# A four-layer decoder trunk on one core: the layer turns and the end of the last layer, written in another order

## The chip, the cores and the metric

The kernel runs on one core of a Trainium2 chip. The metric is the device time of one execution in microseconds (us), the median of several runs. A core has five instruction streams that run side by side and wait for each other by semaphores: PE (TensorE, matrix products and transposes), DVE (VectorE), ACT (ScalarE), POOL (GpSimd) and SP (which here only issues DMAs); ACT and POOL issue DMAs as well. Products of PE land in PSUM, eight banks of 128 x 512 words; everything else lies in SBUF.

## The reference

One sequence of 512 tokens, width 1024, runs through a recurrent (RG-LRU) layer, a PEER expert layer, a multi-head latent attention (MLA) layer, a second PEER layer and a last norm:

```
x = x + gate * rglru(norm(x)*(1+scale)+shift)
x = x + gate * peer(norm(x)*(1+scale)+shift)      # layer 0
k_nope, k_rope, v = shared_kv(x)                  # w_dkv (256), w_kr, latent norm, w_uk, w_uv
x = x + gate * mla(norm(x)*(1+scale)+shift)       # w_dq (384), latent norm, w_uq, 16 heads, w_o
x = x + gate * peer(norm(x)*(1+scale)+shift)      # layer 1
out = rmsnorm(x, final_g)
```

A norm is x * rsqrt(mean(x*x) + eps). PEER makes 8 queries per token (w_pq), takes the top 16 of 128 x 128 product keys for each, and sums over the chosen experts gate * gelu(h . u[e]) * v[e].

## The kernel before, in words

**Layout.** The residual x is kept transposed: 8 tiles k of 128 features by 512 tokens. Every 32-bit product is done as three products of a high and a low half (`mm3`, L188 to L190: weight low by activation high, weight high by activation low, high by high); `split` (L161, L162) makes the halves, the high one as a copy on ACT, the low one as a difference on DVE or POOL. `wtile` loads a weight tile on SP's queue into `raw` and splits it; tiles `whi`, `wlo` come from a small pool, `xhi`, `xlo` from one of the stage. A scheduler orders each engine's stream by its own costs; `tc.issue_after(i)` forces what is inside it behind instruction i.

**A norm** has four steps. `sum_sq` (L221) squares a tile of x on ACT (L226) and adds it to `nacc` on DVE or POOL (L227); `col_sums` (L233) multiplies nacc by ones on PE, one column for each 128 tokens, tile `st`; `rstd_row` takes the square root on ACT (L244), the reciprocal on DVE (L245), and four transposes on PE (L248) that spread it over all partitions, tile `rs`; `normed` (L258) multiplies x by rs, and `affine` (L266 to L274) applies scale and shift, giving `hf` in full and the two halves (`h` in the expert layers, `hmh` and `hml` in attention).

**Stages and turns.** `run` calls `rglru`, `peer(0)`, `mla`, `peer(1)` and `final`. `rglru` ends with the products `wo`, a residual (L283) and the squares. `peer` starts with the norm, three banks `pq` filled k by k with three weight tiles split on DVE, further `pq` groups and scores `sc` (L971). Then two ways are taken: 384 of the tokens go through all 16384 experts densely (tiles u, L188 to L190, with gelu, and gates by the products `wps` of L863, which wait for `pr` on DVE), the last 128 through gathers of the chosen rows (L1169 to L1178). In the value phase 128 steps t add v tiles to the six accumulators `acc` (3 token blocks by 2 halves); the last three steps (`LAST`) are held back and worked off by `emit`, `finish` and the adds of L1143, which turn the token rows `onat` back into columns by PE transposes `ot` (L1121), add the residual and square. In peer two of the eight banks are set apart ("side").

**`mla`** starts with a norm for the keys and one for the queries from the same rs, products `lat` (w_dkv, two tiles) and then `kr` (w_kr), then three more `lat` tiles (w_dq) for the queries. `latent_sums` copies the latents (`latr`), squares them and sums; `latent_norm` (L551) makes ckv and qlat in halves; `values` (v) and `keys` (kn) follow, and per head `q`, `qf` (L654), scores and softmax, `pv` (L695 to L703), and the output products `wo` in four groups g.

**`final`** (L1186) norms x by feature tiles and stores eight tiles of 128 x 512 (L1192, L1193); the host transposes.

## Time and profile before

| | us |
|---|---|
| median of 3 runs | 3069.69 (3067.85 to 3071.66) |
| the profiled execution's own time | 3070.86 |
| its span | 3069.1 |
| PE busy | 2975.9 |
| DVE busy | 2553.9 |
| ACT busy | 1372.3 |
| POOL busy | 899.9 |
| mean granted PE clock | 0.986 |

The profile is of one execution: its span runs from the first to the last instruction, its own time has a little more around it. Rows of groups give a line, an engine, result <- inputs, shapes, the count, then busy time, mean ns of one and the idle time ahead with what ended it. Rows of the timeline give the start, the length, engine, line, operation, and in brackets the engine's wait ahead of it. PE's clock is the share of full speed that the throttle granted.

### The profile page before, as it was taken

To read this page: it belongs to the slowest core of one execution; us is meant where nothing else is said; L and a number is where in the kernel's file an instruction comes from. 1 tells how busy PE (TensorE), PEld (TensorE's weight loads), DVE (VectorE), ACT (ScalarE), POOL (GpSimd) and SP (SyncE) were. 2 spreads that over 40 slices of the span, in tenths; PEclk is the share of its full clock that TensorE was granted. 3 is DMA by queue.
4 is the path that set the end of the run, shared out by engine and by line. 5 is a ranking of instruction groups with operands and counts; after the bars stand their busy time and mean duration, and the time that the engine had idled before them with its cause. 6 is when DMAs were issued, how large, how long until landed. Compare 5 with 4: busy or idle time off the path is not lost.

```text
span 3069.1 us, 43439 instructions
## 1 busy us (share of the span) xinstructions
PE 2975.9 (97%) x15516; PEld 2640.9 (86%) x15516; DVE 2553.9 (83%) x4839; ACT 1372.3 (45%) x1967; POOL 899.9 (29%) x705
## 2 busy tenths in 40 slices
PE   7989999999999999999899989999999999999998
PEld 5679999999888889998677779999999888899986
DVE  8979999898698878879667778999897877788887
ACT  5742255655343333333466642456554333333333
POOL 4000004343224234545333300024342521144441
PEclk9999999999999999999899999999999999999999
DMA  8444568899989999999113344379999999999994
GB/s 311 163 154 145 182 209 311 292 355 317 356 306 378 365 324 350 323 342 328 51 52 121 95 163 130 125 237 325 318 337 330 363 347 331 320 307 353 323 332 145
DMA packets 297209, 814.74 MB, mean 265 GB/s; under 512 B 32864, under 2 KB 131296, under 8 KB 290592
## 3 DMA queue, kind: packets, MB, share of 16 engines
q1 hardware_dynamic: 188912, 438.89, 42.1%
q0 software_dynamic: 78912, 287.34, 26.6%
q10 hardware_dynamic: 29168, 85.72, 7.2%
q8 instruction: 123, 2.02, 0.3%
q14 instruction: 94, 0.77, 0.1%
HBM read 727.70 MB, written 84.15 MB: 265 GB/s over the span
## 4 chain that ended last, share of the span: by engine, by line
PE 74%; DVE 12%; DMA 7%; issue 4%; ACT 2%; POOL 1%; SPq 0%; DVEq 0%; ACTq 0%; POOLq 0%
PE u L188 9%; PE acc L189 9%; PE u L190 9%; PE u L189 9%; PE acc L190 9%; PE acc L188 9%; PE wps L863 5%; DMA vraw<-in_v_dram 3%; DVE wlo L162 2%; DMA ada_raw<-in_adaw_dram 1%; PE pq L188 1%; PE pq L190 1%; PE pq L189 1%; PE ri L415 1%; DVE ada_junk L150 1%
## 5 line engine op out<-in xcount | busy, mean ns | idle before, releaser
L188 PE MATMUL u<-h,wlo 128*128 128x384 f32 x2048 | 691.9, 338 | 1.3 <-ACT gact L928 1.0
L190 PE MATMUL u<-h,whi 128*128 128x384 f32 x2048 | 687.5, 336 | 0.0
L189 PE MATMUL u<-h,whi 128*128 128x384 f32 x2048 | 686.3, 335 | 0.0
L1169 POOL DMA_INDIRECT grow<-in_u_dram,idx x256 | 351.4, 1373 | 1084.2 <-DVE gdot L1173 403.2
L189 PE MATMUL acc<-vl,ah 128*128 128x512 f32 x1536 | 597.8, 389 | 2.7 <-DVE vl L162 2.5
L190 PE MATMUL acc<-vh,ah 128*128 128x512 f32 x1536 | 597.8, 389 | 0.0
L1169 POOL DMA_INDIRECT grow<-in_v_dram,idx x256 | 379.3, 1481 | 652.3 <-DVE gacc L1178 345.7
L188 PE MATMUL acc<-vh,al 128*128 128x512 f32 x1536 | 557.4, 389 | 4.0 <-ACT vh L161 3.4
L162 DVE TENSOR_TENSOR wlo<-raw,whi 128x1024 fp32r<-128x1024 f32 x313 | 382.1, 1222 | 108.4 <-ACT whi L161 108.3
L162 DVE TENSOR_TENSOR vl<-vraw,vh 128x1024 fp32r<-128x1024 f32 x256 | 313.1, 1223 | 144.0 <-ACT vh L161 143.6
L161 ACT ACTIVATE whi<-raw 128x1024 fp32r<-128x1024 f32 (+2 forms) x370 | 356.2, 963 | 149.2 <-issue 38.6
L188 PEld LDWEIGHTS u<-h,wlo 128*128 128x128 f32 x2048 | 386.3, 189 | 5.6 <-ACT gact L928 1.7
L189 PEld LDWEIGHTS u<-h,whi 128*128 128x128 f32 x2048 | 385.6, 188 | 2.7
L190 PEld LDWEIGHTS u<-h,whi 128*128 128x128 f32 x2048 | 385.1, 188 | 0.0
L188 PEld LDWEIGHTS acc<-vh,al 128*128 128x128 f32 x1536 | 288.1, 188 | 64.4 <-ACT vh L161 5.2
L189 PEld LDWEIGHTS acc<-vl,ah 128*128 128x128 f32 x1536 | 288.6, 188 | 61.9 <-DVE vl L162 3.4
L190 PEld LDWEIGHTS acc<-vh,ah 128*128 128x128 f32 x1536 | 288.7, 188 | 59.4
L1178 DVE SCALAR_TENSOR_TENSOR gacc<-grow,gdot,gacc 128x1024 f32<-128x1024 f32 x254 | 325.0, 1279 | 14.6 <-DMA grow<-in_v_dram,idx 13.4
L161 ACT ACTIVATE vh<-vraw 128x1024 fp32r<-128x1024 f32 x256 | 268.7, 1051 | 131.4 <-issue 63.8
L1173 DVE CUSTOM_DVE_ANT_0 grow<-grow,hn 128x1024 f32<-128x1024 f32 x256 | 309.6, 1220 | 16.2 <-DMA grow<-in_u_dram,idx 16.2
L161 ACT ACTIVATE ah<-gact 128x384 fp32r<-128x384 f32 x204 | 106.7, 523 | 361.4 <-PE acc L190 189.2
L863 PE MATMUL wps<-pr,oo 128*128 128x128 f16 x1536 | 191.0, 297 | 14.9 <-DVE pr L856 14.7
(359 smaller groups left out, 4211.5 us busy)
## 6 DMA issues: line engine op xcount, KB each, us to landing
raw<-in_uT_dram SPq DMA_DIRECT2D x256, 512.0 KB, 5.2
vraw<-in_v_dram SPq DMA_DIRECT2D x256, 512.0 KB, 6.2
wscr<-stg ACTq DMA_DIRECT2D x48, 1024.0 KB, 6.6
wt<-wscr SPq DMA_DIRECT2D x14, 3072.0 KB, 19.8
ada_raw<-in_adaw_dram SPq DMA_DIRECT2D x76, 512.0 KB, 4.5
gscr<-gsp ACTq DMA_DIRECT2D x136, 192.0 KB, 5.2
gact<-gscr SPq DMA_DIRECT2D x112, 192.0 KB, 6.6
ada_raw<-in_adaw_dram POOLq DMA_DIRECT2D x36, 512.0 KB, 6.5
```

The source lines that it names most:

```text
L150: nc.vector.tensor_tensor_reduce(junk, raw, self.csil, op0=OP.mult, op1=OP.add, scale=1.0, scalar=b, accum_out=col)
L161: last = nc.scalar.activation(hi, src, AF.Copy)
L162: lo = (eng or nc.vector).tensor_tensor(lo, src, hi.bitcast(F32), op=OP.subtract)
L188: nc.tensor.matmul(out, al, bh, start=first, stop=False)
L189: nc.tensor.matmul(out, ah, bl, start=False, stop=False)
L190: return nc.tensor.matmul(out, ah, bh, start=False, stop=last)
L415: nc.tensor.matmul(out, w[:, q, :], xc[2 * hd + k], start=k == 0, stop=k == 1)
L863: last = nc.tensor.matmul(wps[:, t * P:t * P + P], oo[:, n4 + a, :, t], pr[:, q * n4 + a, :, t], start=q == 0, stop=q == 1)
L1169: nc.gpsimd.indirect_dma_start(out=row, out_offset=None, in_=tabs[s], in_offset=bass.IndirectOffsetOnAxis(ap=idx[:, k:k + 1], axis=0))
L1173: nc.vector.tensor_tensor_reduce(row, row, hn, op0=OP.mult, op1=OP.add, scale=1.0, scalar=0.0, accum_out=col)
L1178: nc.vector.scalar_tensor_tensor(acc, row, col, acc, op0=OP.mult, op1=OP.add)
```

## The change

In the order of the program:

- **Squares and constant products at the turns to peer and mla.** `sum_sq` gets `parts`: the squares of the last two tiles go into a tile `nsq` and are not added to nacc; `col_sums` multiplies nacc and both parts by ones, three times four columns, in an order forced by hand. `fill` puts constant products (128 x 512, f16, of the table iota_e) into PE's stream, ahead of the sums, ahead of the transposes of rs and behind them: 4, 2 and 7 at the two turns to peer, 2, 2 and 7 at the turn to mla. The first products of the stage are held behind the last of them. The three first w_pq tiles are split one after the last residual, one after the last square too, one after the reciprocal and the square root.
- **Entry of attention.** The two w_dkv tiles are loaded and split at the end of peer 0. The three products lat, lat, kr take k in turn; the next xn stands ahead of each low half. Squares of the latents are taken from PSUM, ahead of the copies. The kv sums come after all of lats[1], the third query tile is done in two halves with the transposes of rs between, the query sums stand between the halves of values(0), and their rs ahead of keys(0). The first w_uq and w_uk tiles are split early, on DVE; rope's memset goes from DVE to POOL; the load of the Exp table is later.
- **Exit of attention.** project_out(3) is held behind the last pv product; the last head pair is split on DVE, not POOL.
- **End of layer 1.** `token_major` turns x and the gate g2 into token rows during the value phase (40 transposes on PE, 10 copies on ACT; csil's memory takes the gate). final_g is loaded as rows. `close` works the held steps off block by block: multiply by the gate and add x on DVE, squares with a running sum on ACT, root, reciprocal, product with final_g, and a store of 512 KB of token rows per block, the last one in two halves on two queues. The output is (512, 1024) rows; `final` goes.

```diff
@@ -225,0 +229,7 @@
+        if k >= n - parts:
+            if not self.parts:
+                self.pair_sq = self.wp.tile([P, 2, T], F32, name="nsq", tag="raw", bufs=RAWS)
+            part = self.pair_sq[:, len(self.parts), :]
+            self.parts.append(part)
+            self.last_sq = nc.scalar.activation(part, ch, AF.Square).ins
+            return self.last_sq
@@ -230,6 +240,5 @@
+    def fill(self, bank, n):
+        e = self.iota_e.rearrange("p e t -> p (e t)")
+        for _ in range(n):
+            with self.tc.issue_after(self.tail):
+                self.tail = self.nc.tensor.matmul(bank, e[:, :P], e, start=True, stop=True).ins
@@ -237,3 +246,17 @@
-    def rstd(self, n):
-        self.col_sums()
-        return self.rstd_row(n)
+    def col_sums(self, warm=None):
+        self.sums = self.bank("st")
+        parts, last = [*self.parts[:1], self.nacc, *self.parts[1:]], None
+        if warm:
+            self.fill(self.sums, warm[0])
+            last = self.tail
+        for i, part in enumerate(parts):
+            for b in range(NB):
+                with self.tc.issue_after(last) if last is not None else ExitStack():
+                    last = self.nc.tensor.matmul(self.sums[:, b:b + 1], part[:, b * P:b * P + P], self.ones,
+                                                 start=i + b == 0, stop=i == len(parts) - 1, skip_group_check=True).ins
+        self.tail = last
+        return last
+
+    def rstd(self, n, warm=None):
+        self.col_sums(warm)
+        return self.rstd_row(n, warm)
@@ -248 +273,5 @@
-            nc.tensor.transpose(rs[:, b * P:b * P + P], col[:, 1, b:b + 1].to_broadcast([P, P]), self.ident)
+            with self.tc.issue_after(self.tail) if warm else ExitStack():
+                t = nc.tensor.transpose(rs[:, b * P:b * P + P], col[:, 1, b:b + 1].to_broadcast([P, P]), self.ident)
+        self.tail = t.ins
+        if warm:
+            self.fill(self.sums, warm[2])
@@ -569 +604,3 @@
-            rs = self.rstd(D)
+            last_res, last_sq = self.last_res, self.last_sq
+            rs = self.rstd(D, (2, 2, 7))
+            warm = self.tail
@@ -573,2 +613,4 @@
-                    xn.append(self.normed(hp, k, rs))
-                    hk.append(self.affine(hp, k, xn[k], gk, self.mod[:, 96:104])[1])
+                    step = None
+                    if k + 1 < KC:
+                        step = lambda: xn.append(self.normed(hp, k + 1, rs))
+                    hk.append(self.affine(hp, k, xn[k], gk, self.mod[:, 96:104], between=step)[1])
@@ -577,4 +619,5 @@
-                outs = [self.bank("lat"), self.bank("lat"), self.bank("kr")]
-                self.lin_k(outs[:2], [self.wtile(io["w_dkv"][m], KC, eng=nc.vector) for m in range(2)], hk)
-                self.lin(outs[2], self.wtile(io["w_kr"], KC, eng=nc.vector), hk)
-                wdq = [self.wtile(io["w_dq"][m], KC, pool=hp) for m in range(2)]
+                    with tc.issue_after(warm) if k == 0 else ExitStack():
+                        for out, (hi, lo) in zip(outs, (*self.wdkv, wkr)):
+                            self.mm3(out, (hi[:, k, :], lo[:, k, :]), hk[k], k == 0, k == KC - 1)
+                with tc.issue_after(self.last_sqrt):
+                    wdq = [self.wtile(io["w_dq"][m], KC, pool=hp) for m in range(2)]
@@ -593,4 +636,11 @@
-                with tc.issue_after(self.latent_sums(pool, outs[:2])):
-                    self.lin(lats[1], wdq[1], hq)
-                self.latent_norm("kv_latent_g", ckv)
-                self.lin(lats[2], self.wtile(io["w_dq"][2], KC), hq)
+                self.latent_squares(pool, outs[:2])
+                with tc.issue_after(self.lin(lats[1], wdq[1], hq)):
+                    self.col_sums()
+                w2 = self.wtile(io["w_dq"][2], KC)
+                with tc.issue_after(self.tail):
+                    half = self.lin(lats[2], w2, hq, range(4))
+                with tc.issue_after(half):
+                    rs = self.rstd_row(2 * P)
+                self.latent_norm("kv_latent_g", ckv, rs)
+                with tc.issue_after(self.tail):
+                    whole = self.lin(lats[2], w2, hq, range(4, KC))
@@ -634,2 +684,9 @@
-            values(0)
-            self.latent_sums(top, lats)
+            w0 = self.wtile(io["w_uq"][0], 3, eng=nc.vector)
+            wk0 = self.wtile(io["w_uk"][0], 2, eng=nc.vector)
+            sq = self.latent_squares(top, lats, 1)
+            with tc.issue_after(whole), tc.issue_after(sq):
+                values(0, (0,))
+            with tc.issue_after(self.tail):
+                self.col_sums()
+            with tc.issue_after(self.tail):
+                values(0, (2,))
@@ -743,2 +803,3 @@
-                project_out(3, m)
-                self.sum_sq(pool.tile([P, T], F32, name="sq", tag="t"), self.x[:, m, :], m)
+                with tc.issue_after(self.last_pv):
+                    project_out(3, m)
+                self.sum_sq(pool.tile([P, T], F32, name="sq", tag="t"), self.x[:, m, :], m, parts=2)
@@ -888 +950,3 @@
-                with tc.issue_after(last_nacc), tc.issue_after(last_sq) if m else ExitStack():
+                with ExitStack() as order:
+                    for ins in ((last_res,), (last_res, last_sq), (self.recip, self.last_sqrt))[m]:
+                        order.enter_context(tc.issue_after(ins))
@@ -1100,0 +1170,8 @@
+                if l == DEPTH - 1 and t >= 26 and (t - 26) % 8 == 0 and (t - 26) // 8 <= KC:
+                    with tc.issue_after(grp["v"]):
+                        self.token_major((t - 26) // 8, g2)
+                if l == DEPTH - 1 and t == P - 12:
+                    fg = hpool.tile([P, D], F32, name="fgrow", tag="h4")
+                    with tc.issue_after(vdma[t]):
+                        nc.sync.dma_start(fg, bass.AP(tensor=io["final_g"].tensor, offset=io["final_g"].offset,
+                                                      ap=[[0, P], [1, D]]))
@@ -1106,2 +1186,4 @@
+            if l == 0:
+                with tc.issue_after(vls[-1]), tc.issue_after(self.last_split[0]):
+                    self.wdkv = [self.wtile(io["w_dkv"][m], KC, eng=nc.vector) for m in range(2)]
@@ -1147,0 +1230,62 @@
+    def token_major(self, k, g2):
+        nc = self.nc
+        if k < KC:
+            ot = self.bank("ot", True)
+            for b in range(NB):
+                nc.tensor.transpose(ot[:, b * P:b * P + P], self.x[:, k, b * P:b * P + P], self.ident)
+            nc.scalar.activation(self.x[:, k, :], ot, AF.Copy)
+            return
+        for f in range(2):
+            ot = self.bank("ot", True)
+            for i in range(NB):
+                nc.tensor.transpose(ot[:, i * P:i * P + P], g2[:, f * NB + i:f * NB + i + 1].to_broadcast([P, P]), self.ident)
+            nc.scalar.activation(self.csil[:, f * T:f * T + T], ot, AF.Copy)
+
+    def close(self, pool, acc, held, gathered, fg, splits):
+        nc, tc, io = self.nc, self.tc, self.io
+        nd = NB - 1
+        ys = [pool.tile([P, D], F32, name=f"y{b}", tag=f"h{b}") for b in range(NB)]
+        sq = pool.tile([P, 2, T], F32, name="sqy", tag="h5")
+        st = self.consts.tile([P, NB, 5], F32, name="ssum")
+
+        def add(b, f, src):
+            y = ys[b][:, f * T:f * T + T]
+            nc.vector.tensor_tensor(y, src, self.csil[:, f * T:f * T + T], op=OP.mult)
+            y4 = y.rearrange("p (k n) -> p k n", n=P)
+            last = nc.vector.tensor_tensor(y4, y4, self.x[:, f * NB:f * NB + NB, b * P:b * P + P], op=OP.add).ins
+            nc.scalar.activation(sq[:, f, :], y, AF.Square, accum_out=st[:, b, f:f + 1])
+            if f == 0:
+                nc.vector.tensor_scalar(st[:, b, 2:3], st[:, b, 0:1], 1.0 / D, EPS, op0=OP.mult, op1=OP.add)
+            else:
+                nc.scalar.activation(st[:, b, 3:4], st[:, b, 1:2], AF.Sqrt, bias=st[:, b, 2:3], scale=1.0 / D)
+                nc.vector.reciprocal(st[:, b, 4:5], st[:, b, 3:4])
+            return last
+
+        def out(b, after, parts=1):
+            n = D // parts
+            for i in range(parts):
+                cs = slice(i * n, i * n + n)
+                with tc.issue_after(after):
+                    nc.vector.scalar_tensor_tensor(ys[b][:, cs], ys[b][:, cs], st[:, b, 4:5], fg[:, cs],
+                                                   op0=OP.mult, op1=OP.mult)
+                (nc.scalar if i else nc.sync).dma_start(io["out"][b * P:b * P + P, cs], ys[b][:, cs])
+
+        self.preload(AF.Sqrt, self.last_split[0])
+        last = None
+        for f in range(2):
+            with tc.issue_after(splits[0]), tc.issue_after(splits[1]):
+                after = add(nd, f, gathered[:, f * T:f * T + T])
+        out(nd, after)
+        for b in range(nd):
+            bs = slice(b * P, b * P + P)
+            for f in range(2):
+                fs = slice(f * T, f * T + T)
+                for t, (a, v) in held:
+                    with tc.issue_after(last) if last is not None else ExitStack():
+                        last = self.mm3(acc[b][f], (a[0][:, bs], a[1][:, bs]), (v[0][:, fs], v[1][:, fs]), False,
+                                        t == P - 1).ins
+                after = add(b, f, acc[b][f])
+                if b and f == 0:
+                    out(b - 1, after)
+        out(nd - 1, after, 2)
+
```

Three places in the engines' streams. DVE at the turn from the recurrent layer to peer 0 (`raw` is a loaded weight, wlo and xlo its low half, rcol the reciprocal, xn the normed tile), before:

```order
L227 TENSOR_TENSOR nacc<-nacc,sq 128x512 x3
L162 TENSOR_TENSOR wlo<-raw,whi 128x1024 x3
L162 TENSOR_TENSOR xlo<-raw,xhi 128x1024
L245 RECIPROCAL rcol<-rcol 128x4
L258 TENSOR_TENSOR xn<-x,rs 128x512
L268 TENSOR_SCALAR hf<-xn,gs_f_1540,mod 128x512
```

and after:

```order
L237 TENSOR_TENSOR nacc<-nacc,sq 128x512
L162 TENSOR_TENSOR wlo<-raw,whi 128x1024
L268 RECIPROCAL rcol<-rcol 128x4
L162 TENSOR_TENSOR wlo<-raw,whi 128x1024
L287 TENSOR_TENSOR xn<-x,rs 128x512
L162 TENSOR_TENSOR xlo<-raw,xhi 128x1024
L297 TENSOR_SCALAR hf<-xn,gs_f_1539,mod 128x512
```

Two adds to nacc are gone; the reciprocal stands behind one low half where it stood behind four, and the first xn behind two.

PE in attention, round the query latents' sums (v are value products, kn key products, st the sums), before:

```order
L190 MATMUL v<-wuvh,ckvh_13684 128x256
L233 MATMUL st<-ones,nacc 128x1 x4
L188 MATMUL kn<-ckvh_13682,wlo 128x512
L189 MATMUL kn<-ckvl_13683,whi 128x512
L190 MATMUL kn<-ckvh_13682,whi 128x512
L188 MATMUL kn<-ckvh_13684,wlo 128x512
L189 MATMUL kn<-ckvl_13685,whi 128x512
L190 MATMUL kn<-ckvh_13684,whi 128x512
L248 MATMUL rs<-ident,rcol 128x128 x4
L188 MATMUL q<-qlh_13686,wlo 128x512
```

and after:

```order
L188 MATMUL v<-wuvh,ckvl_13714 128x256
L189 MATMUL v<-wuvl,ckvh_13713 128x256
L190 MATMUL v<-wuvh,ckvh_13713 128x256
L274 MATMUL rs<-ident,rcol 128x128 x4
L188 MATMUL kn<-ckvh_13711,wlo 128x512
L189 MATMUL kn<-ckvl_13712,whi 128x512
L190 MATMUL kn<-ckvh_13711,whi 128x512
L188 MATMUL kn<-ckvh_13713,wlo 128x512
L189 MATMUL kn<-ckvl_13714,whi 128x512
L190 MATMUL kn<-ckvh_13713,whi 128x512
L188 MATMUL q<-qlh_13715,wlo 128x512
```

The transposes of rs now stand ahead of the six key products; the sums themselves moved forward, in among the value products (not in these rows):

```order
L189 MATMUL v<-wuvl,ckvh_13713 128x256
L190 MATMUL v<-wuvh,ckvh_13713 128x256
L255 MATMUL st<-ones,nsq 128x1 x4
L255 MATMUL st<-ones,nacc 128x1 x4
L188 MATMUL v<-wuvh,ckvl_13712 128x256
```

There are two sets of sums, and 12 value products follow them.

DVE at the end (onat are token rows, rest the last quarter's sums, y the token rows of a block, ssum its norm, fo and fgrow the results' scale), before:

```order
L283 SCALAR_TENSOR_TENSOR x<-ot,mod,x 128x512 x3
L1143 TENSOR_TENSOR onat_28514<-onat_28514,rest 128x256
L1143 TENSOR_TENSOR onat_28515<-onat_28515,rest 128x256
L1143 TENSOR_TENSOR onat_28516<-onat_28516,rest 128x256
L283 SCALAR_TENSOR_TENSOR x<-ot,mod,x 128x512 x3
L227 TENSOR_TENSOR nacc<-nacc,sqs 128x512 x3
L245 RECIPROCAL rcol<-rcol 128x4
L1192 SCALAR_TENSOR_TENSOR fo<-x,vecs,rs 128x512 x8
```

and after:

```order
L1255 TENSOR_TENSOR y_28630<-y_28630,x 128x512
L1253 TENSOR_TENSOR y_28631<-acc_23099,csil 128x512
L1253 TENSOR_TENSOR y_28631<-acc_23100,csil 128x512
L1255 TENSOR_TENSOR y_28631<-y_28631,x 128x512
L1261 RECIPROCAL ssum<-ssum 128x1
L1255 TENSOR_TENSOR y_28631<-y_28631,x 128x512
L1269 SCALAR_TENSOR_TENSOR y_28630<-y_28630,ssum,fgrow 128x1024
L1258 TENSOR_SCALAR ssum<-ssum 128x1
L1261 RECIPROCAL ssum<-ssum 128x1
L1269 SCALAR_TENSOR_TENSOR y_28631<-y_28631,ssum,fgrow 128x512 x2
```

The chain of rest, residual, nacc and eight result tiles is gone; the last block's chain is a multiply and an add for each half, with the block before's result queued ahead of the last norm.

More of the change, by code (lines that the diff above doesn't have):

```diff
@@ L189, in mm3, with lin @@
         nc.tensor.matmul(out, ah, bl, start=False, stop=False)
-        return nc.tensor.matmul(out, ah, bh, start=False, stop=last)
-    def lin(self, out, w, acts):
+        last = nc.tensor.matmul(out, ah, bh, start=False, stop=last)
+        self.tail = last.ins
+        return last
+    def lin(self, out, w, acts, ks=None):
         hi, lo = w
         n = len(acts)
-        for k, (bh, bl) in enumerate(acts):
-            last = self.mm3(out, (hi[:, k, :], lo[:, k, :]), (bh, bl), k == 0, k == n - 1)
+        for k in ks or range(n):
+            last = self.mm3(out, (hi[:, k, :], lo[:, k, :]), acts[k], k == 0, k == n - 1)
         return last.ins
@@ L228, in sum_sq, with rstd_row @@
         return self.last_sq
-    def col_sums(self):
-        self.sums = self.bank("st")
-        for b in range(NB):
-            last = self.nc.tensor.matmul(self.sums[:, b:b + 1], self.nacc[:, b * P:b * P + P], self.ones,
-                                         start=True, stop=True)
-        return last.ins
-    def rstd(self, n):
-        self.col_sums()
-        return self.rstd_row(n)
-    def rstd_row(self, n):
+    def fill(self, bank, n):
[4 more added lines that the diff above has]
+    def col_sums(self, warm=None):
+        self.sums = self.bank("st")
+        parts, last = [*self.parts[:1], self.nacc, *self.parts[1:]], None
[12 more added lines that the diff above has]
+        return self.rstd_row(n, warm)
+    def rstd_row(self, n, warm=None):
         nc = self.nc
@@ L1053, in v_load @@
                 else:
-                    vh, vl = (gpool.tile([P, D], F32R, name=n, tag="grow", bufs=GROWS) for n in ("vh", "vl"))
+                    q = 2 * (t - P + 2)
+                    vh, vl = (late[:, (q + i) * D:(q + i + 1) * D] for i in range(2))
                 with ExitStack() as order:
@@ L1184, in gather_steps @@
         yield acc
-    def final(self):
-        nc, io = self.nc, self.io
-        with self.tc.tile_pool(name="fin", bufs=12) as pool:
-            rs = self.rstd(D)
-            for k in range(KC):
-                o = pool.tile([P, T], F32, name="fo", tag="t")
-                nc.vector.scalar_tensor_tensor(o, self.x[:, k, :], self.vec("final_g", k), rs, op0=OP.mult, op1=OP.mult)
-                (nc.sync if k % 2 else nc.scalar).dma_start(io["out"][:, k, :], o)
     def run(self):
```

122 lines of the change are left out of this document (72 added, 50 removed).

## The prediction

> **What bounds the kernel now.** I read the page first, then the waits of TensorE (PE), then the stretches where PE stands still, step by step. The page's first line says that PE is busy nearly all the time, so only the remaining idle time, stretches at a lowered clock, and work that PE need not do can be won.
>
> ```profile
> PE 2975.9 (97%) x15516; PEld 2640.9 (86%) x15516; DVE 2553.9 (83%) x4839; ACT 1372.3 (45%) x1967; POOL 899.9 (29%) x705
> ```
>
> PE idles 3069.1 - 2975.9 = 93.2 us. Its largest waits (total, times, longest) are at the column sums of the norms:
>
> ```profile
> PE st L233 <- DVE nacc L227: 28.2, 7, 13.4
> PE wps L863 <- DVE pr L856: 14.7, 8, 4.5
> ```
>
> The turns from one layer to the next are the place. In windows (length, busy time of PE with instructions, PE load, DVE, ACT, POOL, then PE's granted clock) the turn from the recurrent layer to the first experts shows both losses, idleness and clock:
>
> ```profile
> 183.80:195.00 11.20, 3.01 (x14) 2.58 (x13) 9.75 (x14) 5.18 (x7) 0.00 (x0) 0.62 0.99 362
> 195.00:200.10 5.10, 5.10 (x13) 3.92 (x14) 5.06 (x10) 4.35 (x6) 0.00 (x0) 0.50 0.48 194
> ```
>
> PE works 3.01 of 11.20 us, and for 5.10 us after that its clock is 0.50.
>
> **Turn 1 (recurrent layer to peer 0).** Start, length, engine, line, result, count, and the wait ahead:
>
> ```profile
> 185.15 2.27 DVE L227 TENSOR_TENSOR nacc<-nacc,sq 128x512 f32<-128x512 f32 x3
> 187.34 3.49 DVE L162 TENSOR_TENSOR wlo<-raw,whi 128x1024 fp32r<-128x1024 f32 x3
> 190.75 1.22 DVE L162 TENSOR_TENSOR xlo<-raw,xhi 128x1024 fp32r<-128x1024 f32 x1
> 193.26 0.69 DVE L258 TENSOR_TENSOR xn<-x,rs 128x512 f32<-128x512 f32 x1 [1.21 <-PE rs L248]
> 185.27 0.63 ACT L226 ACTIVATE sq<-x 128x512 f32<-128x512 f32 x1 [0.63 <-DVE x L283]
> 194.95 1.19 PE L188 MATMUL pq<-h,wlo 128*128 128x512 f32 x2 [1.72 <-ACT h L273]
> 215.12 0.40 PE L189 MATMUL pq<-h,whi 128*128 128x512 f32 x1
> 220.36 0.83 PE L971 MATMUL sc<-keys,pq_s 128*128 128x128 f32 x6
> ...
> L161 ACT ACTIVATE whi<-raw 128x1024 fp32r<-128x1024 f32 (+2 forms) x370 | 356.2, 963 | 149.2 <-issue 38.6
> ```
>
> The last square is ready at 185.27 + 0.63 = 185.90, but the reciprocal, which needs it, stands behind all four weight splits, so not before 190.75 + 1.22 = 191.97. In the new order two adds leave DVE and one split stands ahead of the reciprocal. The first weight's high half goes on ACT after that square (963 ns in the page's group), its low half on DVE takes 3.49/3 = 1.16, so the reciprocal is at 185.90 + 0.96 + 1.16 = 188.0, with 0.2 for itself (0.18 in a row below). PE has 2.1 us meanwhile for the sums that wait for the last square. The first xn now stands behind the second weight's low half: ACT makes its high half from about 188.2 (behind the square root) to 189.1, DVE needs 1.16 more, 190.3. From xn to the first product it was 194.95 - 193.26 = 1.69, so products start at 192.0 instead of 194.95: 2.95 earlier. What waits for xn (ACT's h, then the products and everything behind them on PE) is counted in that. The split left over (1.22) now stands ahead of the first hf; what it delays is the second product of the third bank, up to 1.2 us on PE, the other reason for a lower bound. If the constant products keep the clock up, the stretch at 0.50 (5.10 us, worth 2.55) shrinks; the clock steps in its own time, so I take half, 1.3. **Gain 4.2 us (2 to 6).** The constant products (4, 2 and 7) sit in time where PE stood idle; the 7 end the cover only if they run past 192.0, and at half clock, 7 x 0.46 (twice the 0.228 worked out below) = 3.2 us, they do by up to about 1 us: the lower bound.
>
> **The turn peer 0 to attention.**
>
> ```profile
> 1475.68 1.07 DVE L1143 TENSOR_TENSOR onat<-onat,rest 128x256 f32<-128x256 f32 x3
> 1483.75 0.18 DVE L245 RECIPROCAL rcol<-rcol 128x4 f32<-128x4 f32 x1 [2.35 <-ACT rcol L244]
> 1490.58 0.69 DVE L162 TENSOR_TENSOR hml<-hf,hmh 128x512 fp32r<-128x512 f32 x1 [1.55 <-ACT hmh L161]
> 1541.89 2.06 DVE L551 SCALAR_TENSOR_TENSOR latr<-latr,vecs,rs 128x512 f32<-128x512 f32 x3 [3.11 <-PE rs L248]
> 1548.85 0.69 DVE L654 TENSOR_TENSOR qf<-q,rope_t 128x512 f32<-128x512 f32 x1 [1.78 <-PE q L190]
> 1486.77 1.19 PE L188 MATMUL lat<-hmh,wlo 128*128 128x512 f32 x2 [1.67 <-ACT hmh L273]
> 1509.41 0.39 PE L189 MATMUL kr<-hml,whi 128*128 128x512 f32 x1
> 1537.21 1.05 PE L233 MATMUL st<-ones,nacc 128*128 128x1 f32 x8 [0.97 <-DVE nacc L227]
> ```
>
> The low clock and DVE's load, by windows:
>
> ```profile
> 1486.80:1510.00 23.20, 20.23 (x74) 13.98 (x75) 17.43 (x30) 11.69 (x17) 0.56 (x1) 0.92 0.04 14
> 1517.90:1524.70 6.80, 6.80 (x20) 5.64 (x21) 0.18 (x1) 1.49 (x3) 6.18 (x6) 0.51 0.16 49
> 1538.20:1548.90 10.70, 7.75 (x22) 5.63 (x22) 5.53 (x11) 5.18 (x10) 1.82 (x3) 0.68 0.11 31
> ```
>
> First stretch: the adds of rest started 1.3 us late behind a split of the next weights that is now done before; two adds to nacc (2.27/3 = 0.76 each) leave, so the reciprocal comes 2.8 earlier, at 1480.9; the split of w_kr (1.22) lies in the time of the sums. The first product comes at 1484 to 1485, the later when the 7 constant products run at half clock: 1.8 to 2.8 earlier. Second: every odd tile made DVE wait for ACT (1.55 in the row), now the next xn stands there. PE then sets the pace: a wide product takes (220.36 - 215.12)/23 = 0.228 us at full clock (23 products of turn 1 lie between those rows), 74 make 16.9 us instead of 23.2, so the stretch ends near 1502, 8 earlier. Third: 72 products for the query latents (16.4), the kv sums (1.05) and transposes (about 0.6), and 12 half-width value products (1.4) lead to the query sums at 1521.5, where they stood at 1537.21. So 1509.8 to 1537.2, 27.4 us, becomes 19.5; of the 7.9, 3.4 is the stretch at 0.51, the rest waits for norms that now lie behind half of a product group. Fourth: from the sums to qf it was 1548.85 - 1537.21 = 11.6; six products for keys stood ahead of the transposes and go behind them (6 x 0.228 = 1.4); the last split is as late as before. About 10, so qf is near 1531.5. **Gain 17 us (11 to 21)**; the lower end has the clock low in two stretches more, or DVE (17.43 of 23.20 busy) setting the pace. The memset that goes to POOL and the w_uq and w_uk splits that come to DVE (384 and 256 wide) lie in DVE's free time there (0.18 busy of 6.80). The two w_dkv loads move ahead to the end of peer 0 on SP's queue, behind its last value rows:
>
> ```profile
> vraw<-in_v_dram SPq DMA_DIRECT2D x256, 512.0 KB, 6.2
> ```
>
> Such a load lands 6.2 us after its issue, and they have all of the closing products to do so; were they late, their splits would stand in DVE ahead of the residuals as the one did, 1.2 each, and the lower end has that.
>
> **The turn attention to peer 1.**
>
> ```profile
> 1761.50 0.96 PE L188 MATMUL wo<-osh,wlo 128*128 128x512 f32 x3 [2.06 <-ACT osh L161]
> 1772.59 0.39 PE L190 MATMUL wo<-osh,whi 128*128 128x512 f32 x1
> 1782.86 1.22 PE L188 MATMUL pq<-h,wlo 128*128 128x512 f32 x2 [1.63 <-ACT h L273]
> 1761.52 1.28 POOL L162 TENSOR_TENSOR osl<-ot,osh 128x512 fp32r<-128x512 f32 x1 [5.90 <-ACT osh L161]
> 1779.89 0.17 DVE L245 RECIPROCAL rcol<-rcol 128x4 f32<-128x4 f32 x1
> ```
>
> ```profile
> 1782.90:1787.30 4.40, 4.40 (x12) 3.32 (x13) 4.36 (x9) 3.59 (x5) 0.00 (x0) 0.50 1.03 412
> ```
>
> Nine output products that need no last head now fill the 2.06 us; the split of 1.28 on POOL takes 0.69 on DVE (as xn); without the low clock that followed the gap some 8 products save 0.2 each, 1.6. The last product moves from 1772.59 to 1768.8 (3.8). From there the steps are those of turn 1, shown on the old times: the last product ends at 1772.98, a residual (0.75) and a square (0.63) later it is 1774.4, with 0.96 and 1.16 the reciprocal stands at 1776.5 instead of 1779.89; the second split ends at 1776.7 + 0.96 + 1.16 = 1778.8, and 1.69 later, at 1780.5, the products start, not at 1782.86: 2.3. With half of the low stretch (4.40 at 0.50 costs 2.2, half is 1.1): **gain 7 us (4 to 10)**. The lower end has the weights late: the DMA engines show a share of 1.03 in that window, and nothing in the change makes the loads smaller.
>
> **The end.**
>
> ```profile
> 3036.72 0.23 PE acc L188
> 3045.00 0.87 PE ot L1121 x8
> ...
> 3059.80 5.36 DVE L1192 SCALAR_TENSOR_TENSOR fo<-x,vecs,rs 128x512 f32<-128x512 f32 x8 [1.21 <-PE rs L248]
> ...
> L1178 DVE SCALAR_TENSOR_TENSOR gacc<-grow,gdot,gacc 128x1024 f32<-128x1024 f32 x254 | 325.0, 1279 | 14.6 <-DMA grow<-in_v_dram,idx 13.4
> ```
>
> The last result leaves DVE at 3059.80 + 5.36 = 3065.16; the store needs 3.94 more. Now: 3 experts x 6 blocks x 3 = 54 products from 3036.8 take 12.3 us; 40 transposes of token_major, 0.87/8 = 0.109 each, were put on a PE that is busy, so they lengthen the value phase by 4.4. PE ends at 3053.5. Behind it: multiply 0.69, add 0.76, square and root about 1.1, the block before's output 1.28 (the 1279 ns row; DVE has it queued ahead), the last in two halves 2 x 0.7: 5.2, the last store is issued at 3058.7 and ends at 3062.6. Reading the gate and x in (ACT copies) and the load of final_g lie beside PE's work, ACT being at 45%; without that cover nine 0.6 us copies, 5 us. **Gain 6.5 us (4 to 8.5).**
>
> The dense phases get small pieces in another order round the wps products (row of waits above: 14.7 in 8 times): plus or minus 4, taken as 0.
>
> **Rivals.** *The clock does not hold.* At 1537.21 the clock fell a microsecond later although PE had waited only 0.97 us and then done 1.05 us of one-column sums (0.68 in the window from 1538.2). If sums, transposes and small-gap constant products do not hold it, gains are 3 in turn 1, 17 - 3.4 - 1.6 - 3.0 = 9 at attention's entry (the low stretch of 6.80, half of one like it, and 7 constant products at half pace), 7 - 1.1 - 1.6 = 4.3 at its exit and 6.5 at the end: 22.8, **3047**. Chance 0.15: the full-width constant products speak against it. [...]
>
> *The order of the dense phases costs.* If twice the wait for pr arises (14.7 more, less 2), the gain falls to 22: **3047**. Chance 0.07.
>
> *Slower: token_major stops PE.* Its nine pieces stand in PE's queue behind a value product and need x back from memory and a side bank free from ACT. If each stops PE as the last head did (2.06) and a low stretch follows (6.80 at 0.51 costs 3.4, half of that 1.7), 9 x 3.8 = 34 eats the gain, and from 4.5 us per stop the kernel is slower by over 0.2%. Against it: x is loaded six experts ahead of its piece, each 18 products x 0.228 = 4.1 us, so 25 us. Chance 0.07, of which 0.04 slower (near **3080**), 0.03 no difference.
>
> **The numbers.** The forecast: 4.2 + 17 + 7 + 6.5 = 34.7. The profiled execution took 3070.86 with a span of 3069.1 (1.8 around it), so 3036.2; the median of the three, 3069.69, is 1.2 less: **3035**. Its chance is 0.71, its own range with the terms' ends partly cancelling 3025 to 3044. A range to 3049 takes in the two rivals near 3047, down to 3023 the upper ends. A measurement can tell about 0.2%, 6.1 us, from no change: faster 0.93 (forecast and two rivals), same 0.03, slower 0.04.
>
> **What would show it.** Right: the first pq product near 192.0 at turn 1, and 7 to 8 us behind the last wo product instead of 10.27 at the third turn; the first latent products with no DVE wait for ACT above 0.5; qf some 51 us behind its turn's reciprocal instead of 65 (1548.85 - 1483.75); the last store issued about 5 us behind the last product; PE's idle time near 70. Wrong: a clock of 0.5 for over 3 us right after a turn (first rival), waits of wps above 20 (second), waits of ot in the last value phase (third), or a last store no earlier than 3064.

## The result and the profile after

The changed kernel takes 3054.11 us (median of 6, 3044.84 to 3056.83); the kernel before took 3070.46 (median of 6). The ratio is 0.9943, 95% interval 0.9932 to 0.9953: about 17 us faster (14 to 21). The forecast was 3035 with a range down to 3023 and up to 3049: right in direction, and about half of the gain is missing. The profiled execution spans 3055.1 us, 14.0 less than before; all stage numbers below are its own. One execution among all the runs below is left out of the times: 3285.19 us, of old_peer_turns, at a mean granted clock of 0.847.

The page after, PE's row, and PE's largest waits:

```profile
PE 2982.9 (98%) x15578; PEld 2647.2 (87%) x15578; DVE 2552.6 (84%) x4838; ACT 1378.3 (45%) x1982; POOL 882.8 (29%) x699
```
```profile
PE wps L924 <- DVE pr L917: 17.3, 8, 3.9
PE st L255 <- DVE nacc L237: 13.3, 1, 13.3
```

PE idles 72.2 us instead of 93.2, as forecast (near 70), and the waits at the sums fell from 28.2 to 13.3, the part of the very first norm. But the same page has PE 7.0 us busier: the constant products and the further sums and transposes are work too, and idle time that they fill is not time won. Turn 1, by the timeline after (SP's loads, ACT's high halves, PE):

```profile
182.58 8.93 SPq L175 DMA_DIRECT2D raw<-in_w_pq_dram  x4
...
189.77 1.06 ACT L161 ACTIVATE whi<-raw 128x1024 fp32r<-128x1024 f32 x1 [2.35 <-DMA raw<-in_w_pq_dram]
192.23 1.06 ACT L161 ACTIVATE whi<-raw 128x1024 fp32r<-128x1024 f32 x1 [0.81 <-DMA raw<-in_w_pq_dram]
197.11 1.06 ACT L161 ACTIVATE xhi<-raw 128x1024 fp32r<-128x1024 f32 x1 [3.83 <-DMA raw<-in_w_pq_dram]
...
184.93 0.39 PE L190 MATMUL wo<-yh,whi 128*128 128x512 f32 x1
199.02 0.71 PE L188 MATMUL pq<-h,wlo 128*128 128x512 f32 x2 [2.69 <-ACT h L305]
225.82 0.39 PE L1036 MATMUL sc<-keys,pq_s 128*128 128x128 f32 x2
```

ACT waits for the weights to land: 2.35, 0.81 and 3.83 us. Before, SP issued the same four loads 26 us earlier:

```profile
156.11 14.74 SPq L175 DMA_DIRECT2D raw<-in_w_pq_dram  x4
...
183.42 0.39 PE L190 MATMUL wo<-yh,whi 128*128 128x512 f32 x1
```

From the last wo product to the scores it was 220.36 - 183.42 = 36.9 us and is 225.82 - 184.93 = 40.9. The third turn after:

```profile
1758.15 0.50 PE L188 MATMUL wo<-osh,wlo 128*128 128x512 f32 x1 [2.80 <-POOL wlo L162]
1759.41 0.45 PE L190 MATMUL wo<-osh,whi 128*128 128x512 f32 x1
1760.71 1.86 PE L244 MATMUL st<-iota_e 128*128 128x512 f16 x4 [0.84 <-DVE x L315]
1762.37 1.70 PE L255 MATMUL st<-ones,nsq 128*128 128x1 f32 x8
1771.64 1.42 PE L188 MATMUL pq<-h,wlo 128*128 128x512 f32 x2
1795.43 1.50 PE L1036 MATMUL sc<-keys,pq_s 128*128 128x128 f32 x12
```

PE waits 2.80 us for the low half of the last w_o tile, the clock falls (0.50 from 1762 to 1770, rows in the last section), and from the last wo product to the first pq product it is 12.2 us instead of 10.3. The entry of attention and the end are near the forecast:

```profile
1537.04 0.69 DVE L714 TENSOR_TENSOR qf<-q,rope_t 128x512 f32<-128x512 f32 x1
...
3033.61 0.39 PE L188 MATMUL acc<-vh,al 128*128 128x512 f32 x1
3045.83 0.39 PE L190 MATMUL acc<-late,ah 128*128 128x512 f32 x1
3050.09 1.41 DVE L1269 SCALAR_TENSOR_TENSOR y<-y,ssum,fgrow 128x512 f32<-128x512 f32 x2
```

Last, PE's waits at the start of layer 1's value phase (2300 to 2470 us), after:

```profile
PE acc L188 <- DVE al L162: 3.6, 2, 2.0
PE acc L188 <- ACT vh L161: 2.5, 1, 2.5
```

and before:

```profile
PE acc L188 <- ACT vh L161: 0.8, 1, 0.8
```

### The profile page after: what moved, and what is told of

Same layout as the page of the kernel before. It is cut to its first block, busy times and chain, and to the rows that moved or that the text cites. A ratio compares the mean times of both kernels' runs of the same rounds, so it can differ in the third digit from the quotient of the medians.

```text
span 3055.1 us, 43505 instructions
## 1 busy us (share of the span) xinstructions
PE 2982.9 (98%) x15578; PEld 2647.2 (87%) x15578; DVE 2552.6 (84%) x4838; ACT 1378.3 (45%) x1982; POOL 882.8 (29%) x699
## 4 chain that ended last, share of the span: by engine, by line
PE 81%; DVE 10%; DMA 5%; issue 3%; ACT 1%; POOL 1%; SPq 0%; DVEq 0%; ACTq 0%; POOLq 0%
PE acc L188 11%; PE acc L189 11%; PE acc L190 11%; PE u L188 9%; PE u L190 9%; PE u L189 9%; PE wps L924 5%; DVE wlo L162 2%; DMA ada_raw<-in_adaw_dram 1%; PE pq L189 1%; PE pq L190 1%; PE pq L188 1%; DMA vraw<-in_v_dram 1%; PE ri L447 1%; PE tp L743 1%
## 5 line engine op out<-in xcount | busy, mean ns | idle before, releaser
L190 PE MATMUL acc<-vh,ah 128*128 128x512 f32 x1512 | 589.4, 390 | 0.0
L189 PE MATMUL acc<-vl,ah 128*128 128x512 f32 x1512 | 589.2, 390 | 0.0
L1313 POOL DMA_INDIRECT grow<-in_v_dram,idx x256 | 370.5, 1447 | 661.8 <-DVE gacc L1322 379.8
L188 PE MATMUL acc<-vh,al 128*128 128x512 f32 x1512 | 550.6, 390 | 7.2 <-DVE al L162 3.6
L162 DVE TENSOR_TENSOR wlo<-raw,whi 128x1024 fp32r<-128x1024 f32 (+1 forms) x315 | 385.0, 1223 | 122.1 <-ACT whi L161 121.7
L927 ACT ACTIVATE stg<-wps 128x512 f32<-128x512 f32 x192 | 187.7, 1110 | 46.2 <-PE wps L924 39.1
## 6 DMA issues: line engine op xcount, KB each, us to landing
gscr<-gsp ACTq DMA_DIRECT2D x136, 192.0 KB
gact<-gscr SPq DMA_DIRECT2D x112, 192.0 KB
```

The lines of the kernel that those rows point to most:

```text
L162: lo = (eng or nc.vector).tensor_tensor(lo, src, hi.bitcast(F32), op=OP.subtract)
L188: nc.tensor.matmul(out, al, bh, start=first, stop=False)
L189: nc.tensor.matmul(out, ah, bl, start=False, stop=False)
L190: last = nc.tensor.matmul(out, ah, bh, start=False, stop=last)
L927: nc.scalar.activation(stg[:, :, c:c + 4].rearrange("p e t -> p t e"), wps.rearrange("p (t e) -> p t e", t=4), AF.Copy, scale=1.0 / GSCALE)
L1313: nc.gpsimd.indirect_dma_start(out=row, out_offset=None, in_=tabs[s], in_offset=bass.IndirectOffsetOnAxis(ap=idx[:, k:k + 1], axis=0))
```

## The experiments

Ratios are to the kernel before, measured beside each, with 95% intervals; the gain is (1 - ratio) x 3070. "Waits" are PE's waits for acc between 2300 and 2470 us in that kernel's profile, and "loads" the value loads that stand on SP ahead of the first read of the gates (`wt`) in layer 1.

| kernel | median | ratio | gain | waits | loads |
|---|---|---|---|---|---|
| changed | 3054.11 | 0.9943 (0.9932 to 0.9953) | 17.5 | 6.1 | 4 |
| changed_again | 3055.90 | 0.9953 (0.9939 to 0.9967) | 14.4 | 6.0 | 4 |
| loads_first | 3041.90 | 0.9918 (0.9901 to 0.9935) | 25.2 | 4.1 | 4 |
| turn1_load | 3040.59 | 0.9907 (0.9894 to 0.9920) | 28.6 | 2.4 | 2 |
| third_turn_load | 3047.16 | 0.9921 (0.9907 to 0.9935) | 24.3 | 4.9 | 4 |
| no_fill | 3053.59 | 0.9955 (0.9939 to 0.9972) | 13.8 | 3.1 | 3 |
| loads_no_fill | 3050.16 | 0.9934 (0.9920 to 0.9947) | 20.3 | 1.5 | 2 |
| gscr_later | 3052.93 | 0.9954 (0.9938 to 0.9971) | 14.1 | 3.7 | 4 |
| value_start_order | 3038.29 | 0.9894 (0.9879 to 0.9909) | 32.5 | 5.3 | 3 |
| gates_first | 3050.02 | 0.9937 (0.9924 to 0.9950) | 19.3 | 1.1 | 2 |
| loads_and_gates_first | 3038.20 | 0.9899 (0.9885 to 0.9913) | 31.0 | 0.5 | 2 |
| old_peer_turns | 3050.47 | 0.9949 (0.9933 to 0.9964) | 15.7 | 2.7 | 3 |
| end_only | 3064.92 | 0.9976 (0.9967 to 0.9985) | 7.4 | 3.8 | 3 |
| old_end | 3051.43 | 0.9940 (0.9927 to 0.9954) | 18.4 | 2.2 | 2 |
| entry_only | 3061.20 | 0.9966 (0.9952 to 0.9979) | 10.4 | 1.7 | 2 |
| entry_and_late | 3055.73 | 0.9961 (0.9949 to 0.9974) | 12.0 | 6.5 | 3 |

**The late loads.** The theory after the first profile: the w_pq loads stand behind two ada loads (weights of the norms' scale and shift) on SP, and `nsq`, which takes one of the four `raw` buffers, delays the last w_o tile. The edit of loads_first, its first half turn1_load, its second third_turn_load:

```diff
-        nc.sync.dma_start(r, ap)
+        self.last_raw = nc.sync.dma_start(r, ap).ins
...
+            first_pq = self.last_raw
...
-                    with tc.issue_after(last):
+                    with tc.issue_after(last), tc.issue_after(first_pq):
                         self.adas(6 if l == 0 else 2, pool)
...
-                self.sum_sq(pool.tile([P, T], F32, name="sq", tag="t"), self.x[:, m, :], m, parts=2)
+                if m:
+                    self.sum_sq(pool.tile([P, T], F32, name="sq", tag="t"), self.x[:, m - 1, :], m - 1, parts=2)
+            self.sum_sq(pool.tile([P, T], F32, name="sq", tag="t"), self.x[:, m, :], m, parts=2)
```

> The changed kernel with two loads put ahead again: SP issues the first three w_pq loads of each expert layer ahead of the ada loads, and the last w_o tile takes its buffer ahead of nsq. Theory (late loads): at turn 1 the wait of ACT for w_pq (2.35, 0.81 and 3.83 us in the trace) and at the third turn the wait of PE for the last w_o split (2.80) go; the first pq product at turn 1 moves from 199.0 to about 196.3, where the seven constant products then end; with the clock stretch behind it some 4 us there and 2.8 at the third turn: 3047 to 3049. Rival (the clock falls at the turns whatever the loads do): the same time, 3052 to 3056.

> The changed kernel with only the first half of loads_first: SP issues the first three w_pq loads of each expert layer ahead of the ada loads. In the traces the pq products of turn 1 came 5.5 us later than before in the changed kernel and 1.3 earlier in loads_first. Theory (turn 1's part of the gain of 12 is some 6 to 7): 3047 to 3049. Rival (turn 1's gain is taken back at the end of layer 0, where the gathers set the pace, and all of it came at the third turn): 3052 to 3056.

> The changed kernel with only the second half of loads_first: the last w_o tile takes its buffer ahead of nsq. In the traces the third turn gained 4.6 us in loads_first and lost 2.2 in the changed kernel. Theory: 3048 to 3051. Rival (only turn 1 counts): 3053 to 3056.

All three are faster than the changed kernel, by 7 to 14 us by the ratios, and more than expected: loads_first and turn1_load by 5 to 6 us, third_turn_load by under one. Their intervals lie clear of changed_again's; those of loads_first and third_turn_load touch the changed kernel's first one. In turn1_load SP's loads, the last wo product, the high halves, the sums, the first pq product and the scores:

```profile
161.38 9.48 SPq L175 DMA_DIRECT2D raw<-in_w_pq_dram  x3
180.11 0.80 SPq L146 DMA_DIRECT2D ada_raw<-in_adaw_dram  x2
...
183.44 0.39 PE L190 MATMUL wo<-yh,whi 128*128 128x512 f32 x1
185.82 1.98 ACT L161 ACTIVATE whi<-raw 128x1024 fp32r<-128x1024 f32 x2
188.52 1.85 PE L255 MATMUL st<-ones,nsq 128*128 128x1 f32 x8
190.41 0.26 ACT L267 ACTIVATE rcol<-st,eps 128x4 f32<-128x4 f32 x1 [2.60 <-PE st L255]
194.46 0.70 PE L188 MATMUL pq<-h,wlo 128*128 128x512 f32 x2
217.51 2.84 PE L1037 MATMUL sc<-keys,pq_s 128*128 128x128 f32 x24
```

ACT waits for no weight, and the turn takes 217.51 - 183.44 = 34.1: 2.9 less than before, 6.8 less than changed. What ACT's square root waits for now are the sums on PE. In third_turn_load the wait of the wo products for a low half is 0.5:

```profile
PE wo L188 <- POOL wlo L162: 0.5, 1, 0.5
```

The third turn, from the last pv product to the scores, takes 44.3 us there, for 51.1 in the changed kernel and 48.9 before. The two together give no more than the first alone (the intervals overlap). By the profiles loads_first has both turns short, 33.9 and 44.3, and loses in layer 1 what it won: PE waits 6.4 us for pr at the wps products and 4.1 at the start of the value phase, where turn1_load waits 3.3 and 2.4. Of turn1_load's 11 to 14 us over the changed kernel, its turn shows 6.8, the wps products of layer 1 3.7 (3.3 for 7.0) and the start of the value phase 3.7; why the last two went with the loads of layer 0 is not shown.

**The constant products.** no_fill issues none; loads_no_fill does so on loads_first.

```diff
-        for _ in range(n):
+        for _ in range(0):
```

> The changed kernel without any constant products. Theory (they lie in series with the sums and hold no clock): turn 1 stays, since w_pq is late there anyway; at the third turn the sums start 1.7 us earlier and the first pq product waits for h alone, some 2 us, at attention's entry up to 2: 3049 to 3052. Rival (they do hold the clock): each of the three turns has one more stretch of 3.4 us at half clock, 1.7 each: 3057 to 3060.

> The kernel of loads_first without the constant products. Once the loads are early, one theory (the constant products keep or bring the clock up at the turns) expects the first pq product of turn 1 about 1.5 us earlier, since nothing is queued ahead of it, but a stretch of 3.4 us more at half clock at each of the three turns, 1.7 each: 3043 to 3046. The other (they only lengthen PE's queue ahead of the sums and the first products): 3037 to 3040.

The 3.4 us of both expectations is the shortest low stretch in the trace of the kernel before: there the clock is 0.50 from 1538.25 to 1541.67 and from 1545.08 to 1548.49, and 1.00 between; at its turn 1 it is 0.50 from 186.58 to 200.23.

While the weights are late the constant products make no difference that shows. Where the loads are early, 4.9 us go with them by the ratios, more than either theory gave, but the two intervals overlap (0.9901 to 0.9935 and 0.9920 to 0.9947). By the profiles the three turns are 6.2 us longer without them: turn 1 34.9 for 33.9, from the first latent product to qf 51.6 for 48.5, the third turn 46.5 for 44.3. Layer 0's value phase (first to last acc product), where no constant product lies, differs by still more, 676.6 for 668.4, and nothing here explains that. The third turn in windows, with them (loads_first):

```profile
1749.00:1753.00 4.00, 3.88 (x30) 3.08 (x28) 2.18 (x2) 2.98 (x5) 0.00 (x0) 1.00 0.79 196
1753.00:1757.00 4.00, 3.68 (x12) 2.10 (x13) 3.52 (x7) 1.75 (x3) 0.00 (x0) 0.57 1.06 439
1757.00:1761.00 4.00, 4.00 (x21) 3.16 (x20) 3.96 (x8) 3.43 (x6) 0.00 (x0) 1.00 0.96 402
```

and without (loads_no_fill):

```profile
1765.00:1769.00 4.00, 3.20 (x26) 3.15 (x27) 1.49 (x3) 2.60 (x4) 0.00 (x0) 0.89 0.72 179
1769.00:1773.00 4.00, 1.68 (x6) 1.15 (x5) 3.68 (x5) 2.05 (x3) 0.00 (x0) 0.50 1.07 432
1773.00:1777.00 4.00, 3.91 (x11) 2.55 (x10) 3.96 (x8) 3.37 (x5) 0.00 (x0) 0.50 0.93 394
```

One window is low with them (0.57), and two are without (0.50). In loads_first PE was busy for 3.68 of the 4.00 us of the low window, and the next has the clock at 1.00. In the changed kernel's third turn PE is fully busy from 1762 to 1770, 4.00 of 4.00 us twice, and the clock stays at 0.50 (last section). Nor does busy time tell when it falls: 3.88 of 4.00 stood ahead of the 0.57.

**The start of layer 1's value phase.** There gates (wt), kept activations (gscr) and value rows are read on SP's one queue. Edits: each gscr read behind the value load of the step before (gscr_later); this, and the fourth value load behind the gates, on loads_first (value_start_order); two value loads alone ahead of the gates (gates_first on the changed kernel, loads_and_gates_first on loads_first):

```diff
...
-                vdma.append(nc.sync.dma_start(raw, io["v"][l * P + t]).ins)
+                with tc.issue_after(grp["wdma"]) if t == 2 else ExitStack():
+                    vdma.append(nc.sync.dma_start(raw, io["v"][l * P + t]).ins)
```

> The changed kernel, each read of a kept activation (gscr) forced behind the value load of the step before on SP's queue. Theory (a read that waits for its buffer for 11.3 us holds three value loads behind it): the waits of acc at the start of layer 1's value phase (6.1 us) shrink to under 2: 3049 to 3051. Rival (the DMA engines are full there, share 1.0): the same time within 2 us, 3052 to 3056.

> The kernel of loads_first with SP's order at the start of the value phases put back: the fourth value load behind the first read of the gates, and each read of a kept activation behind the value load of the step before. Theory (the order on SP delays the gates, wt, and the value loads): the waits of acc at the start of layer 1's value phase, 4.1 us, shrink to about 1: 3037 to 3039. Rival (the DMA engines are full there and the same bytes come no sooner): 3041 to 3043.

> The changed kernel with one order put back on SP: at the start of a value phase two value loads stand ahead of the first read of the gates, where the changed kernel has four in layer 1. In the profiles so far PE's waits for acc at that place sum to 1.5 to 2.4 us where two loads stand ahead (4 profiles), 0.8 to 5.3 with three (6) and 3.7 to 6.1 with four (5). Theory (each load ahead holds the gates back): waits of about 2 instead of 6, 3050 to 3052. Rival (the number of loads goes along by chance, the DMA engines are full): the same time as the changed kernel, 3054 to 3056.

> loads_first with the same order at the start of the value phase (two value loads ahead of the gates). loads_first had four there and waits of 4.1 us. Theory: 3037 to 3040, with all three causes of the shortfall gone, near the forecast of 3035. Rival: 3041 to 3043.

> The kernel before once more, for a second profile of it: whether the start of layer 1's value phase waits as little as the 0.8 us of the first profile (then the changed kernel's 6 us are its own), or 3 and more.

In the changed kernel's trace one gscr read, at 2382.27, holds SP for 11.34 us with three value loads behind it, and the DMA engines' share is 1.00 from 2400 to 2470. The gscr reads are not the cause: gscr_later's rival holds. value_start_order's time came out as its theory said, but its profile (of the slowest of its four executions) still waits 5.3, so it does not show the cause. gates_first does for the waits: 1.1 us, where the two profiles of the changed kernel have 6.1 and 6.0,

```profile
PE acc L188 <- DVE al L162: 0.6, 1, 0.6
PE acc L188 <- ACT vh L161: 0.5, 1, 0.5
```

and by the table the waits are short with two loads ahead, 0.5 to 2.4; three and four do not separate, 2.7 to 6.5 and 3.7 to 6.1. The time does not show it: gates_first's interval overlaps the changed kernel's, and loads_and_gates_first's overlaps that of loads_first. The waits are not the changed kernel's alone: the kernel before has three loads ahead, and its first profile waits 0.8, its second (one time, 3073.95) 3.9.

```profile
PE acc L188 <- DVE al L162: 2.3, 1, 2.3
PE acc L188 <- ACT vh L161: 1.6, 1, 1.6
```

**The parts alone.** old_peer_turns undoes both turns to peer; end_only has only the new end; old_end is loads_first without it; entry_only has the entry of attention, and entry_and_late adds the buffer `late`. This buffer is part of the changed kernel, though the list of the change does not name it: the value halves of the last two steps lie in the gates' memory and no longer in buffers of the gathered rows. end_only has it too, old_end does not. The edit from entry_only to entry_and_late:

```diff
-                    vh, vl = (gpool.tile([P, D], F32R, name=n, tag="grow", bufs=GROWS) for n in ("vh", "vl"))
+                    q = 2 * (t - P + 2)
+                    vh, vl = (late[:, (q + i) * D:(q + i + 1) * D] for i in range(2))
...
```

> The changed kernel with the two turns to peer as before (all squares to nacc, no constant products, the old order of the w_pq splits and of project_out, the last head's split on POOL); the entry of attention and the end stay new. Theory (these two turns lose 5.5 and 2.2 us in the changed kernel, and the order on SP that stops the value phase comes with them): 3042 to 3047. Rival (they win what was forecast, 4 and 7, and something else ate it): 3062 to 3066.

> The kernel before with the new end of layer 1 alone (token_major, close, final_g as rows); all turns are the old ones. In the changed kernel the end gains 11 us behind the last u products, 3.8 are given back by the 40 transposes, and 3 to 5 at the start of the value phase, in each kernel so far that has the new turn into attention and the new end. Theory (that stall comes from arriving earlier at the value phase than the gates can be read back): no stall here, the gain is 7: 3060 to 3062. Rival (it comes from the new code of layer 1, by the order of the loads or the buffers): a gain of 3 to 4: 3064 to 3066.

> The kernel of loads_first with the old end of layer 1 (rest, finish and final; no token_major). Theory (the end is worth 11 less 3.8, the stall at the value phase comes with the early arrival and stays): 3048 to 3050. Rival (the stall belongs to the new code of layer 1 and goes): 3044 to 3046.

> The kernel before with the new entry of attention alone (early w_dkv, squares and constant products at that turn, the interleaved products, the reordered latent chain); the turns to peer and the end are the old ones. Forecast: 17, and the traces of the changed kernels show 17 to 20 from the end of layer 0's value phase to the first scores: 3050 to 3053. Rival (some of it is given back at the value phase, by the early arrival): 3054 to 3057.

> entry_only with the last two steps' value halves in the buffer of the gates (late) and not in the gathers' rows. entry_only gained 9 where the turn shows 13 in its own trace, and it did not win the 6 us between layer 0's last value steps and the first latent product that the changed kernel wins. Theory (the held steps waited for gather rows, so the early w_dkv splits behind them came late): 3054 to 3057. Rival (those 6 us come from elsewhere): 3060 to 3062.

> The changed kernel once more, for its spread and as the measure of the other kernels of this call: 3052 to 3056; and whether its value phase of layer 1 stops for 6 us in another execution too, or for as little as the 0.8 that the kernel before showed.

Without the two turns the kernel is as fast as with them, between the two theories by its time: together they bring nothing while their loads are late (15.7 without them, 25.2 with them in loads_first). The end with `late` is worth 7.4, on loads_first 6.8 (25.2 - 18.4), near the forecast 6.5; but part of both lies in layer 0's value phase, where `late` is in use: end_only takes 672.6 there for 676.4 and 675.0 in the two profiles before, old_end 675.7 for 668.4. entry_only misses the forecast; at the end of layer 0 the last value halves wait on ACT for buffers of gathered rows, and PE waits for `al`, which stands on DVE behind the two w_dkv splits (2.35 us from 1464.81):

```profile
1456.85 1.06 ACT L161 ACTIVATE vh<-vraw 128x1024 fp32r<-128x1024 f32 x1 [1.93 <-DVE gacc L1241]
1460.81 1.06 ACT L161 ACTIVATE vh<-vraw 128x1024 fp32r<-128x1024 f32 x1 [2.89 <-DVE gacc L1241]
...
1467.68 0.80 PE L188 MATMUL acc<-vh,al 128*128 128x512 f32 x1 [4.05 <-DVE al L162]
1491.37 0.82 PE L188 MATMUL lat<-hmh,wlo 128*128 128x512 f32 x2
```

In entry_and_late these waits are gone and the first latent product comes 10.85 earlier:

```profile
1480.52 0.81 PE L188 MATMUL lat<-hmh,wlo 128*128 128x512 f32 x2
```

Its execution spans 3052.7, 16.4 less than before, with 6.5 us of waits at the value phase; the ratio gives 12.0. The traces bear the mechanism out; the times do not separate the two kernels, whose intervals overlap almost wholly.

## Why the prediction was wrong, step by step

**Turn 1, forecast 4.2 gained, measured 4.0 lost: the first failed step.** "The first weight's high half goes on ACT after that square" took the weight as loaded. In the new order the loads stand behind the ada loads, and ACT waits for them, 2.35, 0.81 and 3.83 us. The step left out SP's stream, though the change holds the splits back and so moves their loads. With the loads early (turn1_load) the turn gains 2.9, inside the stated 2 to 6, but not by the forecast's path. "PE has 2.1 us meanwhile for the sums" was too little: the last square is done at 185.92, and the sums, behind four constant products, end at 190.37. So the first pq product comes at 194.46 and not near 192.0, 0.5 earlier than before and not 2.95; the other 2.4 are won behind it, at a higher clock (1.00 from 195 to 200, where it was 0.50 before). That the sum fits its range is luck.

**The third turn, forecast 7 gained, measured 0.6 lost** from the last wo product to the scores (36.0 for 35.4), and 1.5 from the last pv to the last wo: **the second failed step.** "Nine output products ... now fill the 2.06 us" is right, but the gap came back as 2.80 us of waiting for the last w_o tile, because `nsq` uses its buffer; and "the lower end has the weights late" thought of w_pq. A constant product was costed as idle time filled; at the fallen clock (0.50) four of them and three sets of sums take 1760.71 to 1767.48 in series ahead of the root. With that load early (third_turn_load) the turn gains 4.6 from the last pv product to the scores, inside 4 to 10; the first pq product is then 9.3 behind the last wo product, not 7 to 8. The forecast's 3.8 up to the last wo product was not quite the sum of its own parts, 2.06, 0.6 and 1.6.

**The entry, forecast 17: 13.1 at its place.** qf is at 1537.04, 11.8 earlier than before, from a start 5.5 late: 17.3, and it follows the turn's reciprocal by 53.2, near the forecast 51. But from layer 0's last acc product to qf it is 66.2 for 79.3, 13.1. The other 4.2 lie in layer 0: its value phase is 6.5 shorter, to which the buffer `late` belongs, and the experts ahead of it take 2.4 more. The prediction counted both at nothing, so the agreement with 17 is partly luck. By the times the entry alone gives 10.4, with `late` 12.0. The first latent product came at 1487.08, not 1484 to 1485.

**The end, forecast 6.5: right.** From the first held product to the end of the span it is 3055.1 - 3033.6 = 21.5 instead of 3069.1 - 3036.6 = 32.5, less the 4.4 counted for the transposes: 6.6 in the profile. The 7.4 and 6.8 of the times contain `late`.

**The dense phases, taken as 0 within 4.** The sum left out SP's order at the start of the value phase: PE waits 6.1 us there, for 0.8 and 3.9 in the two profiles before, so this costs 2.2 to 5.3 us.

**The rivals.** That the clock does not hold was given 0.15. Its sign, a clock near 0.5 for over 3 us right after a turn, came at turn 1 (0.59 and 0.56 in the windows 199 to 203 and 203 to 207); at the third turn the clock was low during the sums (0.50 from 1762 to 1770), and at attention's entry it held (0.98 from 1486 to 1503); with the loads early, the constant products leave one low window (0.57) at the third turn where there are two (0.50) without them. In its sum the 3.0 at attention's entry follows from no row shown. Costly dense phases came true, but on SP, not at the wps products (17.3 for 14.7). token_major stops nothing: no wait for ot in the value phase.

With both sets of loads and the gates put right, loads_and_gates_first takes 3038.20, and is faster than the kernel before and the changed kernel. Its gain of 31.0 is near the forecast 34.7, but 7.0 of it, by its profile, lie in layer 0's value phase (669.4 for 676.4), which the forecast took as 0.

## What to carry to other kernels

When a step is held back or gets a buffer from a shared ring, follow its loads on the DMA queue before counting the compute chain: here holding splits back moved their loads by 26 us. Read each queue's order at both ends of a stage, since a change elsewhere may put other loads ahead of what is waited for. Constant products stand in series with what is queued behind them (at the changed kernel's third turn four of them and the sums took 6.8 us ahead of the root): here they paid at most where the weights behind them were loaded, 4.9 us by the ratios with intervals that overlap. And compare a part's gain at its own place in the trace, not only in the total, where other stages add to it or take from it.

## What was not expected of the hardware

PE was fully busy and still at a low clock: in loads_first from 189 to 193, 4.00 of 4.00 us busy with sums, constant products and transposes, clock 0.59, after a window with 2.52 of 4.00 busy.

```profile
185.00:189.00 4.00, 2.52 (x19) 1.80 (x17) 2.96 (x6) 2.67 (x4) 0.00 (x0) 1.00 0.98 393
189.00:193.00 4.00, 4.00 (x22) 3.22 (x22) 2.62 (x4) 1.69 (x3) 0.00 (x0) 0.59 1.00 396
```

In the changed kernel's third turn it lasted longer, with the same work on PE:

```profile
1762.00:1766.00 4.00, 4.00 (x20) 3.91 (x19) 1.23 (x1) 0.27 (x1) 0.00 (x0) 0.50 0.77 218
1766.00:1770.00 4.00, 4.00 (x16) 2.79 (x17) 1.42 (x3) 1.21 (x2) 0.00 (x0) 0.50 1.04 438
```

So PE's busy time alone does not set the clock in these windows. What kept it low there, no run here separates.
